# Subtracting the low halves of all split weights on VectorE instead of GpSimd, in a two-layer hybrid decoder kernel

## The chip, the cores and the metric

The kernel runs on one core of a Trainium2 chip. The metric is the device time of one execution in microseconds (us); of several runs the median is given. TensorE is PE in the profile, VectorE is DVE, ScalarE is ACT, GpSimd is POOL, SyncE is SP. PEld is TensorE's weight load.

## The reference

Two layers of a decoder trunk, 512 tokens of width 1024, all in float32. Per layer:

```python
h = rmsnorm(x, norm_g)
proj = h @ w_in                          # 1024 x 11168
a_b, a_c, a_x, a_z, c_q, c_kv, k_pe, b_z, dq, dk, dv, c_z, gate_pre = split(proj)
# A: gated depthwise convolution over 3 tokens
y_a = a_b * (conv_b + sum(up[tap] * conv_w[tap])) * silu(a_z)      # up: shifted a_c * a_x
# B: causal latent attention, 8 heads: q from c_q, k and v from c_kv, rotary key k_pe
y_b = attention(rope(rmsnorm(rmsnorm(c_q) @ w_uq)), rmsnorm(rmsnorm(c_kv) @ w_ukv)) * silu(b_z)
# C: dilated window attention, 3 groups of 8 heads (dilation 1, 4, 16), merged by their log-sums
y_c = dilated(rmsnorm(dq), rmsnorm(dk), dv) * silu(c_z)
merged = sum(sigmoid(gate_i) * (y_i @ w_out_i) for i in (a, b, c))
x = x + merged @ w_o
```

## The kernel before

Every product with a weight matrix is made of three matmuls on split numbers: a float32 value is a high half (a copy rounded to fp32r) and a low half (the value minus its high half). `mm3` (L123 to L128) issues hi·hi, hi·lo and lo·hi. The activations' halves are `hhi` and `hlo` (8 slices of 128x512); the weights come tile by tile.

A weight tile is fetched and split by `split_weights` (L108 to L122). SP issues the DMA into `wraw` (5 buffers, 128x1024), ACT copies it into `whi` (L120, 5 buffers), and another engine subtracts `whi` from `wraw` into `wlo` (L121, 5 buffers). Which engine that is, is chosen by `pool=`. Without the argument it is POOL (`W_POOL = 1`); this holds for all projection tiles through `proj_t` (conv tiles, z tiles, gate tiles), for the `w_out` tiles of the gates and for `w_o`: 136 tiles of 128x1024. The four tiles of 128x768 of each dilated group (24 groups) go to POOL for q in `G_POOL = (0, 2)` and to DVE for the others. The low-rank tiles (128x832) and those of the latent attention are on DVE.

POOL has more work. In layer 0 it adds the squares of x into `acc` (L210), where DVE does it in layer 1. It subtracts the odd slices of `hlo` (L290), the low halves of v (L434), and it scales: k rows (L437), probabilities (L480), the dilated q and k (L596).

The order of PE's instructions is written out by hand. `filler()` yields projection steps (conv tiles, four z tiles, 12 dilated groups, a last conv tile, four z tiles, the gates), and the main line of the layer places a number of them (`F_LORA`, `F_P1` and others) between the small steps of the latent attention, so that PE has matmuls while the other engines normalise and do the softmax. The queues of DVE, ACT, POOL and SP are ordered by the scheduler from priorities, `split_weights` being given 250 steps ahead (`W_AHEAD`), except for the first loads of layer 0, whose DVE, ACT and SP orders are by hand too (from L264). Each engine works through its queue in order.

Steps that come up below, in the order of the program:

- Layer 0's start: `take_chunk` splits x (L211, L212) and sums its squares (L210); `row_scale` sums over partitions on PE (L254), reads that on DVE (L257), and takes the reciprocal root by small DVE steps (`rsqrt`, L98 to L106); PE then spreads the result over rows by L284, and DVE makes h from it (L287).
- The latents: `lat` is normalised (L320, L321) and transposed by PE (L345).
- The latent attention's q and k: `mla_p1` ends with a root and a scaling on DVE (L428), and PE transposes them (L455). Its softmax: DVE L476 and L479, POOL L480, PE L491.
- The convolution's taps on DVE: L823 to L839.
- A dilated group: squares summed on DVE (L590), a root, the scaling on POOL (L596), and PE's transposes (L608).

Of the kernel before, what the change touches and what calls it, by code (L numbers as in the profile page):

```python
# [14 lines left out]
P = 128  # L15
S = 512
# [7 lines left out]
FAR = 1e30  # L24
HIGHEST = 3e38
W_AHEAD = 250
W_POOL = 1
G_POOL = (0, 2)
C8, C2, W_RAW, W_BUF = 2, 38, 5, 5

F_LORA, F_P1, F_P2, F_MLA, F_TAIL, N_TAIL = 24, 6, 10, 1.2, 5.0, 28
# [16 lines left out]
def hybrid_kernel(ctx: ExitStack, tc: tile.TileContext, a: dict):  # L48
    nc = tc.nc
# [7 lines left out]

    ctx.enter_context(tc.manual_schedule(engines={mybir.EngineType.PE}))
    uid = [0]
    wcount = [0]  # L60
    wlast = [None]

    def nm(s):
# [12 lines left out]
    def small(shape, tag, bufs=2):  # L76
        return sp.tile(shape, F32, tag=tag, name=nm(tag), bufs=bufs)
# [15 lines left out]
    hhi = hp.tile([P, KD, S], F32R, name="hhi")  # L93
    hlo = hp.tile([P, KD, S], F32R, name="hlo")
# [10 lines left out]
            nc.vector.tensor_tensor(out=t, in0=t, in1=y, op=ALU.mult)  # L105
            nc.vector.scalar_tensor_tensor(out=y, in0=t, scalar=1.5, in1=y, op0=ALU.add, op1=ALU.mult)  # L106

    def split_weights(n, dmas, pool=None, parts=1):  # L108
        with tc.high_priority(offset=max(0, min(W_AHEAD, tc.cur_priority - base[0]))):
            raw = wp.tile([P, 1024], F32, tag="wraw", name=nm("wraw"), bufs=W_RAW)  # L110
            for lo_, hi_, view, src in dmas:
                wlast[0] = nc.sync.dma_start(view(raw[:, lo_:hi_]), src)
            hi = wp.tile([P, 1024], F32R, tag="whi", name=nm("whi"), bufs=W_BUF)
            lo = wp.tile([P, 1024], F32R, tag="wlo", name=nm("wlo"), bufs=W_BUF)
            wcount[0] += pool is None
            on_pool = wcount[0] % W_POOL == 0 if pool is None else pool
            eng = nc.gpsimd if on_pool else nc.vector
            for i in range(parts):
                c = slice(i * n // parts, (i + 1) * n // parts)
                nc.scalar.copy(hi[:, c], raw[:, c])  # L120
                eng.tensor_sub(lo[:, c], raw[:, c], hi[:, c])  # L121
        return hi, lo  # L122

    def mm3(out, lhs, rhs, start, stop):
# [67 lines left out]
                after_weights(dma)  # L192
        return prm, ropeg

    def new_x(first=False):

        return {"x": [], "hi": [], "lo": [], "acc": small([P, S], "acc", 1), "first": first}

    def take_chunk(X, k, prm):
        src = X["x"][k]  # L200
        hi, lo = t2([P, S], F32R), t2([P, S], F32R)
        X["hi"].append(hi)
        X["lo"].append(lo)
        g = prm[:, O_NORM + k:O_NORM + k + 1]
        if k == 0:
            nc.scalar.activation(X["acc"], src, AF.Square)
        else:
            sq = t2([P, S])
            nc.scalar.activation(sq, src, AF.Square)
            (nc.gpsimd if X["first"] else nc.vector).tensor_add(X["acc"], X["acc"], sq)  # L210
        nc.scalar.activation(hi, src, AF.Copy, scale=g)  # L211
        nc.vector.scalar_tensor_tensor(out=lo, in0=src, scalar=g, in1=hi, op0=ALU.mult, op1=ALU.subtract)  # L212

# [4 lines left out]
    for _ in range(N_WAKE):  # L218
        nc.tensor.matmul(ps[:, :P], wake, wake, start=True, stop=True)

    X = new_x(first=True)
    base = [1 << 40]

    for l in range(DEPTH):
# [6 lines left out]
        wl = {}  # L231

        def lora_w(k):
            n = W_LORA
            dmas = [(0, 2 * n, lambda t: t.rearrange("p (k n) -> p k n", k=2), w_in[:, k:k + 2, C_LORA:C_LORA + n])]
            if l == 0 and k == 0:
                dmas = [(i * n, (i + 1) * n, lambda t: t, w_in[:, i, C_LORA:C_LORA + n]) for i in range(2)]
            wl[k // 2] = split_weights(2 * n, dmas, pool=False, parts=len(dmas))

        def lora(k0, k1):  # L240
            for k in range(k0, k1):
# [43 lines left out]
        for k in range(KD):  # L285
            h32 = t2([P, S])
            nc.vector.scalar_tensor_tensor(out=h32, in0=X["x"][k], scalar=prm[:, O_NORM + k:O_NORM + k + 1],  # L287
                                           in1=psr, op0=ALU.mult, op1=ALU.mult)
            nc.scalar.copy(hhi[:, k], h32)
            (nc.gpsimd if k % 2 else nc.vector).tensor_sub(hlo[:, k], h32, hhi[:, k])  # L290
        lora(n1, n2)
        if l == 0:
            base[0] = tc.cur_priority
# [74 lines left out]
        mla = {}  # L368

        def mla_prep_w(p):  # L370

            o = 0 if p % 2 else 768
            dmas = [(o, o + 256, lambda t: t, w_ukv[:, p * 256:(p + 1) * 256])]
            if p % 2 == 0:
                dmas.insert(0, (0, 768, lambda t: t.rearrange("p (k n) -> p k n", k=2),
                                w_uq[:, :, p * 192:(p + 2) * 192]))
            mla[p] = {"w": split_weights(o + 256, dmas, pool=False)}

        def mla_p1(p):
            m = mla[p]  # L380
# [173 lines left out]
        w_dil = w_in[:, :, C_DIL:C_DIL + 4608].rearrange("p k (s n) -> p k s n", s=3)  # L554
        dil = {}

        def dil_group(p, g):
            if g == 0:
                bias = sp.tile([P, 2, S], F32, tag="bias", name=nm("bias"), bufs=1)
                after_weights(nc.sync.dma_start(bias, a["bias"][2 * p:2 * p + 2].rearrange("h p n -> p h n")))  # L560
                dil[p] = {"bias": bias, "qkt": [], "v": [], "nat": []}
            m = dil[p]
            c0 = g * 512 + p * P
            wq = []
            for q in range(4):
                wq.append(split_weights(768, [
                    (k * 384, k * 384 + 384, lambda t: t.rearrange("p (s n) -> p s n", s=3),
                     w_dil[:, 2 * q + k, :, c0:c0 + P]) for k in range(2)], pool=q in G_POOL))
            both = t8([P, 2, NCH, 256])
            nat, sq = both[:, 0], both[:, 1]  # L570
            vt = t2([P, NCH, P])
            m["nat"].append(nat)
            m["v"].append(vt)

            def evac(c, ps):
                nc.scalar.copy(nat[:, c], ps[:, 0:256])
                nc.scalar.copy(vt[:, c], ps[:, 256:384])

            yield from proj_n(wq, 384, evac)
            if g == 0:  # L580

                vscr = dp.tile([S, P], F32, tag="vscr", name=nm("vscr"))
                nc.sync.dma_start(vscr.rearrange("(r p) d -> p r d", p=P), vt)
                nc.sync.dma_start(vt, vscr.rearrange("(p c) d -> p c d", p=P))
            s2 = small([P, 16], "s16a")
            v2 = small([P, 16], "s16b")
            r2 = small([P, 16], "s16c")
            for c in (0, 2):
                nc.scalar.activation(sq[:, c:c + 2], nat[:, c:c + 2], AF.Square)
                nc.vector.reduce_sum(s2[:, 4 * c:4 * c + 8], sq[:, c:c + 2].rearrange("p c (h d) -> p (c h) d", d=64), axis=AX.X)  # L590
            nc.vector.tensor_scalar(out=v2, in0=s2, scalar1=1.0 / 64, scalar2=EPS, op0=ALU.mult, op1=ALU.add)
            rsqrt(r2, v2, [P, 16])
            nv = nat.rearrange("p c (h d) -> p (c h) d", d=64)
            eng = nc.gpsimd if NV_POOL else nc.vector
            for i in (0, 8):
                eng.tensor_tensor(out=nv[:, i:i + 8], in0=nv[:, i:i + 8],  # L596
                                  in1=r2[:, i:i + 8].unsqueeze(2).to_broadcast([P, 8, 64]), op=ALU.mult)
# [353 lines left out]
        if not last:  # L951
            prm, ropeg = load_params(l + 1, later=True)
            X = new_x()
# [106 lines left out]
```

## Time and profile before

| | before |
|---|---|
| median of 3 runs | 1499.07 us (1498.89 to 1502.35) |
| profiled execution | 1497.07 us, its span 1495.3 us |
| mean granted TensorE clock | 0.988 of full speed |
| PE busy | 1451.1 us (97%) |
| DVE busy | 797.4 us (53%) |
| ACT busy | 699.3 us (47%) |
| POOL busy | 559.5 us (37%) |
| DMA queue q1 | 32.3% of 16 engines' span |

The span is the part of the execution that the profiler's events cover. Busy time is the time in which an engine has an instruction of its own running. That includes time in which the running instruction is held up, so a long duration of a small instruction is itself a sign of waiting. The figure in brackets at the end of a timeline row is the idle time before it and what ended it.

### The profile page before, as it was taken

The numbers are of one execution on the slowest core, as the hardware profiler recorded it, in microseconds if no ns is written. First come the engines' busy times: TensorE is split into PE (matmuls) and PEld (weight loads), VectorE is DVE, ScalarE is ACT, GpSimd is POOL, SyncE is SP. The second block draws the span as 40 slices with busy tenths as digits, with TensorE's granted clock in tenths as the row PEclk, the third lists the DMA queues.
The fourth block names the chain that finished last, engine by engine and source line by source line (L and its number), as shares of the span: only waits on it lengthen the run. The fifth ranks groups of instructions, "written<-read, shape, count | busy, mean of one in ns | idle before, by whom it ended". The sixth has DMA issues, their size and how long they took to land. (4 is left out here: it accounts for less than half of the span.)

```text
span 1495.3 us, 21490 instructions
## 1 busy us (share of the span) xinstructions
PE 1451.1 (97%) x7838; PEld 1272.1 (85%) x7838; DVE 797.4 (53%) x2120; ACT 699.3 (47%) x1600; POOL 559.5 (37%) x348
## 2 busy tenths in 40 slices
PE   8989999999999999999999899999999999999998
PEld 8777899999888878888898778999999878788887
DVE  7757776556464742221665767756474746412221
ACT  4545566647464532232444455657565544322220
POOL 6434243232225434444243433332222434344441
PEclk8999999999999999999999999999999999999999
DMA  8131223234243333333532311234233433233322
GB/s 242 50 95 47 53 68 82 76 85 115 54 124 99 87 85 96 91 104 106 171 101 74 92 36 43 67 85 115 66 92 106 109 91 86 85 99 96 106 81 85
DMA packets 235706, 136.34 MB, mean 91 GB/s; under 512 B 18000, under 2 KB 227280, under 8 KB 235600
## 3 DMA queue, kind: packets, MB, share of 16 engines
q1 hardware_dynamic: 235600, 134.96, 32.3%
q8 instruction: 62, 1.02, 0.3%
q14 instruction: 44, 0.36, 0.1%
HBM read 128.45 MB, written 6.49 MB: 90 GB/s over the span
## 5 line engine op out<-in xcount | busy, mean ns | idle before, releaser
L121 POOL TENSOR_TENSOR wlo<-wraw,whi 128x1024 fp32r<-128x1024 f32 (+1 forms) x184 | 424.7, 2311 | 627.8 <-ACT whi L120 607.2
L120 ACT CAST whi<-wraw 128x1024 fp32r<-128x1024 f32 (+4 forms) x249 | 235.3, 949 | 360.5 <-issue 195.0
L126 PE MATMUL pj<-hhi,whi 128*128 128x512 f32 x760 | 307.8, 405 | 0.2
L127 PE MATMUL pj<-hlo,whi 128*128 128x512 f32 x760 | 298.8, 393 | 0.0
L128 PE MATMUL pj<-hhi,wlo 128*128 128x512 f32 x760 | 298.7, 393 | 0.0
L126 PE MATMUL pj<-whi,hhi 128*128 128x384 f32 x768 | 272.2, 354 | 0.0
L128 PE MATMUL pj<-whi,hlo 128*128 128x384 f32 x768 | 258.4, 336 | 0.0
L127 PE MATMUL pj<-wlo,hhi 128*128 128x384 f32 x768 | 257.6, 335 | 0.0
L128 PEld LDWEIGHTS pj<-hhi,wlo 128*128 128x128 f32 x760 | 143.8, 189 | 31.3
L126 PEld LDWEIGHTS pj<-hhi,whi 128*128 128x128 f32 x760 | 144.3, 190 | 28.1 <-issue 1.4
L127 PEld LDWEIGHTS pj<-hlo,whi 128*128 128x128 f32 x760 | 144.4, 190 | 24.3 <-POOL hlo L290 0.3
L879 DVE SCALAR_TENSOR_TENSOR c<-c,sc 128x512 f32<-128x512 f32 x48 | 32.7, 684 | 239.9 <-PE sc L128 239.9
L126 PEld LDWEIGHTS pj<-whi,hhi 128*128 128x128 f32 x768 | 145.0, 189 | 5.7 <-issue 2.1
L127 PEld LDWEIGHTS pj<-wlo,hhi 128*128 128x128 f32 x768 | 145.2, 189 | 0.6
L128 PEld LDWEIGHTS pj<-whi,hlo 128*128 128x128 f32 x768 | 144.4, 188 | 0.0
L674 ACT ACTIVATE c<-c,e 128x128 f32<-128x128 f32 (+1 forms) x192 | 79.9, 417 | 46.6 <-DVE e L671 46.6
L121 DVE TENSOR_TENSOR wlo<-wraw,whi 128x768 fp32r<-128x768 f32 (+3 forms) x65 | 77.8, 1197 | 42.4 <-ACT whi L120 25.5
L480 POOL TENSOR_SCALAR c<-c,mst 128x128 f32<-128x128 f32 (+1 forms) x64 | 35.5, 555 | 134.9 <-DVE mst L479 100.2
L596 POOL TENSOR_TENSOR c<-c,s16c 128x512 f32<-128x512 f32 x48 | 49.1, 1043 | 91.3 <-DVE s16c L106 91.3
L126 PE MATMUL sc<-c,whi 128*128 128x512 f32 x192 | 75.5, 393 | 0.0
L128 PE MATMUL sc<-c,wlo 128*128 128x512 f32 x192 | 74.9, 390 | 0.0
L127 PE MATMUL sc<-c,whi 128*128 128x512 f32 x192 | 74.8, 390 | 0.0
(201 smaller groups left out, 2367.1 us busy)
## 6 DMA issues: line engine op xcount, KB each, us to landing
wraw<-w_in SPq DMA_DIRECT2D x96, 512.0 KB, 3.7
wraw<-w_in SPq DMA_DIRECT2D x192, 192.0 KB, 2.8
wraw<-w_o SPq DMA_DIRECT2D x16, 512.0 KB, 4.2
bias<-bias SPq DMA_DIRECT2D x8, 512.0 KB, 3.5
wraw<-w_out_a SPq DMA_DIRECT2D x8, 512.0 KB, 3.3
wraw<-w_out_b SPq DMA_DIRECT2D x8, 512.0 KB, 3.3
wraw<-w_out_c SPq DMA_DIRECT2D x8, 512.0 KB, 3.4
wraw<-w_in SPq DMA_DIRECT2D x7, 416.0 KB, 3.7
```

The costliest lines, as they stand in the source:

```text
L120: nc.scalar.copy(hi[:, c], raw[:, c])
L121: eng.tensor_sub(lo[:, c], raw[:, c], hi[:, c])
L126: nc.tensor.matmul(out, lhs[0], rhs[0], start=start, stop=False)
L127: nc.tensor.matmul(out, lhs[0], rhs[1], start=False, stop=False)
L128: nc.tensor.matmul(out, lhs[1], rhs[0], start=False, stop=stop)
L480: nc.gpsimd.tensor_scalar(out=pr[:, :n_], in0=pr[:, :n_], scalar1=st[:, 3:4], scalar2=1.0, op0=ALU.mult, op1=ALU.mult)
L596: eng.tensor_tensor(out=nv[:, i:i + 8], in0=nv[:, i:i + 8], in1=r2[:, i:i + 8].unsqueeze(2).to_broadcast([P, 8, 64]), op=ALU.mult)
L674: nc.scalar.activation(dst, dst, AF.Exp, bias=mc, scale=-1.0, accum_out=sc_)
L879: nc.vector.scalar_tensor_tensor(out=ths[e], in0=ths[e], scalar=1.0, in1=ps, op0=ALU.add, op1=ALU.mult)
```

## The change

The low halves of all split weights are subtracted on DVE: the argument `pool=` and the constants `W_POOL` and `G_POOL` are gone. So are the `first` flag of `new_x`, by which layer 0's sums of squares went to POOL, and the choice of POOL for the odd slices of `hlo`. POOL keeps L434, L437, L480 and L596 (by the numbering of before) and the fills.

```diff
-    def split_weights(n, dmas, pool=None, parts=1):
+    def split_weights(n, dmas, parts=1):
...
-            wcount[0] += pool is None
-            on_pool = wcount[0] % W_POOL == 0 if pool is None else pool
-            eng = nc.gpsimd if on_pool else nc.vector
             for i in range(parts):
                 c = slice(i * n // parts, (i + 1) * n // parts)
                 nc.scalar.copy(hi[:, c], raw[:, c])
-                eng.tensor_sub(lo[:, c], raw[:, c], hi[:, c])
+                nc.vector.tensor_sub(lo[:, c], raw[:, c], hi[:, c])
...
-            (nc.gpsimd if X["first"] else nc.vector).tensor_add(X["acc"], X["acc"], sq)
+            nc.vector.tensor_add(X["acc"], X["acc"], sq)
...
-            (nc.gpsimd if k % 2 else nc.vector).tensor_sub(hlo[:, k], h32, hhi[:, k])
+            nc.vector.tensor_sub(hlo[:, k], h32, hhi[:, k])
...
-                     w_dil[:, 2 * q + k, :, c0:c0 + P]) for k in range(2)], pool=q in G_POOL))
+                     w_dil[:, 2 * q + k, :, c0:c0 + P]) for k in range(2)]))
```

PE's instructions and their order are the same in both. POOL's queue goes from 329 to 130 rows and DVE's from 2000 to 2206; the 199 instructions are 184 of L121, 8 of L290 and 7 of L210. ACT's copies and SP's loads shift by a few places. The lines of the changed kernel are numbered lower: L121 is L115 there, and what stands behind it in the file is lower by 6.

DVE's queue in layer 0's start, before. L121 is the last low-rank tile's subtraction; L257 reads the sum of squares, and L104 to L106 are the root, which ends with the second L106; L287 needs the result through PE's L284.

```order
L121 TENSOR_TENSOR wlo_195<-wraw_192,whi_194 128x832
L305 TENSOR_TENSOR rt_370<-cos_76,ropeg_107 128x128 x2
L212 SCALAR_TENSOR_TENSOR c_52_199<-c_44_183,prm_106,c_51_198 128x512
L257 TENSOR_SCALAR nv_274<-tr_269 128x4
...
L101 TENSOR_SCALAR rs_i_277<-nv_274 128x4
L306 TENSOR_TENSOR rt_370<-sin_77,ropeg_107 128x128
L102 TENSOR_SCALAR nr_275<-rs_i_277 128x4
L104 SCALAR_TENSOR_TENSOR rs_t_278<-nr_275,nv_274 128x4
...
L106 SCALAR_TENSOR_TENSOR nr_275<-rs_t_278,nr_275 128x4
L287 SCALAR_TENSOR_TENSOR c_60_320<-c_9_104,prm_106,tr_315 128x512
```

And now:

```order
L115 TENSOR_TENSOR wlo_195<-wraw_192,whi_194 128x832
L204 TENSOR_TENSOR acc_96<-acc_96,c_53_200 128x512
L206 SCALAR_TENSOR_TENSOR c_52_199<-c_44_183,prm_106,c_51_198 128x512
L251 TENSOR_SCALAR nv_274<-tr_269 128x4
L299 TENSOR_TENSOR rt_370<-cos_76,ropeg_107 128x128
...
L102 TENSOR_TENSOR rs_t_278<-rs_t_278,nr_275 128x4
L103 SCALAR_TENSOR_TENSOR nr_275<-rs_t_278,nr_275 128x4
L115 TENSOR_TENSOR wlo_429<-wraw_426,whi_428 128x1024
L101 SCALAR_TENSOR_TENSOR rs_t_278<-nr_275,nv_274 128x4
...
L103 SCALAR_TENSOR_TENSOR nr_275<-rs_t_278,nr_275 128x4
L115 TENSOR_TENSOR wlo_461<-wraw_458,whi_460 128x1024
L115 TENSOR_TENSOR wlo_502<-wraw_499,whi_501 128x1024
L115 TENSOR_TENSOR wlo_543<-wraw_540,whi_542 128x1024
L281 SCALAR_TENSOR_TENSOR c_60_320<-c_9_104,prm_106,tr_315 128x512
```

The two L305 pairs no longer stand ahead of the last L212, the sum of squares (L204) does; one weight subtraction (`wlo_429`) lies inside the root, and three more (`wlo_461`, `wlo_502`, `wlo_543`) between the root and the first L281 (was L287). On POOL those four were rows of its own queue.

DVE's queue ahead of the first scaling of q in layer 0, before: the end of a conv tile's taps (L837) and the sums from which the root of `mla_p1` is taken (L418 to L101).

```order
L837 SCALAR_TENSOR_TENSOR c_111_601<-c_110_600,prm_106,c_111_601 128x256
L837 SCALAR_TENSOR_TENSOR c_111_601<-c_110_600,prm_106,c_111_601 128x2x96
L837 SCALAR_TENSOR_TENSOR c_111_601<-c_110_600,prm_106,c_111_601 128x2x28
L837 SCALAR_TENSOR_TENSOR c_111_601<-c_110_600,prm_106,c_111_601 128x2x3
L418 TENSOR_REDUCE s24a_623<-c_142_758 128x8
L333 TENSOR_TENSOR c_145_777<-c_116_621,rt_370 128x256
...
L422 TENSOR_SCALAR s24b_624<-s24a_623 128x24
L335 TENSOR_TENSOR c_116_621<-c_145_777 128x4x2x16
```

And now:

```order
L831 SCALAR_TENSOR_TENSOR c_111_601<-c_110_600,prm_106,c_111_601 128x256
L115 TENSOR_TENSOR wlo_951<-wraw_948,whi_950 128x1024
L831 SCALAR_TENSOR_TENSOR c_111_601<-c_110_600,prm_106,c_111_601 128x2x96
...
L831 SCALAR_TENSOR_TENSOR c_111_601<-c_110_600,prm_106,c_111_601 128x2x3
L412 TENSOR_REDUCE s24a_623<-c_142_758 128x8
L327 TENSOR_TENSOR c_145_777<-c_116_621,rt_370 128x256
...
L833 TENSOR_TENSOR c_111_601<-pj_746,c_111_601 128x512
L416 TENSOR_SCALAR s24b_624<-s24a_623 128x24
L115 TENSOR_TENSOR wlo_1078<-wraw_1075,whi_1077 128x1024
L98 TENSOR_SCALAR rs_i_764<-s24b_624 128x24
```

Two weight subtractions, `wlo_951` and `wlo_1078`, which were on POOL, now lie in this chain, the first inside the taps, the second between L416 (was L422) and the root's first step L98 (was L101); the tap's product L833 (was L839) comes ahead of the root.

DVE's queue at the second conv tile's taps, in the softmax stretch of layer 0, before (L479 is a reciprocal of the softmax, L181 a low half of the probabilities, `s24d` the second root of `mla_p1`):

```order
L827 TENSOR_TENSOR c_159_865<-pj_954,c_159_865 128x512
L102 TENSOR_SCALAR s24d_931<-rs_i_990 128x8
L828 TENSOR_SCALAR c_160_866<-c_159_865,prm_106 128x512
L104 SCALAR_TENSOR_TENSOR rs_t_991<-s24d_931,s24b_930 128x8
L837 SCALAR_TENSOR_TENSOR c_160_866<-c_159_865,prm_106,c_160_866 128x384
...
L479 RECIPROCAL mst_1052<-mst_1052 128x1
L181 TENSOR_TENSOR c_203_1039<-tr_1060,c_202_1038 128x2x128
L106 SCALAR_TENSOR_TENSOR s24d_931<-rs_t_991,s24d_931 128x8
```

And now:

```order
L821 TENSOR_TENSOR c_159_865<-pj_954,c_159_865 128x512
L99 TENSOR_SCALAR s24d_931<-rs_i_990 128x8
L115 TENSOR_TENSOR wlo_1380<-wraw_1377,whi_1379 128x1024
L101 SCALAR_TENSOR_TENSOR rs_t_991<-s24d_931,s24b_930 128x8
L473 RECIPROCAL mst_1052<-mst_1052 128x1
...
L102 TENSOR_TENSOR rs_t_991<-rs_t_991,s24d_931 128x8
L822 TENSOR_SCALAR c_160_866<-c_159_865,prm_106 128x512
L103 SCALAR_TENSOR_TENSOR s24d_931<-rs_t_991,s24d_931 128x8
```

`wlo_1380` comes in behind L99 (was L102), and the first tap L822 (was L828) now stands behind the reciprocal L473 (was L479) and behind the next L175 (was L181) and not ahead of them.

## Rows read from the trace of the kernel before

**Rows 1.** Page, part 1: busy time, share of the span, instructions of each engine.

```profile
PE 1451.1 (97%) x7838; PEld 1272.1 (85%) x7838; DVE 797.4 (53%) x2120; ACT 699.3 (47%) x1600; POOL 559.5 (37%) x348
```

**Rows 2.** Waits: who waited for whom, us in total, times, longest.

```profile
PE tr L455 <- DVE c L428: 10.5, 4, 4.1
PE tr L608 <- POOL c L596: 9.7, 11, 1.9
PE tr L284 <- issue: 4.8, 1, 4.8
PE tr L491 <- DVE s24d L106: 3.8, 2, 1.9
PE tr L345 <- DVE c L320: 3.6, 1, 3.6
...
ACT whi L120 <- PE pj L127: 124.8, 44, 5.2
```

**Rows 3.** Stretches: from:to, length, busy (instructions) PE, PEld, DVE, ACT, POOL, clock, DMA.

```profile
100.00:300.00 200.00, 194.44 (x1164) 178.19 (x1164) 134.14 (x399) 124.81 (x326) 70.24 (x71) 0.99 0.25 67
575.00:755.00 180.00, 180.00 (x796) 149.17 (x795) 52.09 (x67) 56.18 (x70) 71.28 (x29) 1.00 0.40 120
```

**Rows 4.** Groups by form: count, busy us, mean ns, idle before and its releasers.

```profile
L121 POOL TENSOR_TENSOR wlo<-wraw,whi 128x1024 fp32r<-128x1024 f32 x136 | 335.5, 2470 | 406.7 <-ACT whi L120 388.8 <-issue 12.6 <-DMA wraw<-w_in 3.4
L121 POOL TENSOR_TENSOR wlo<-wraw,whi 128x768 fp32r<-128x768 f32 x48 | 89.2, 1859 | 221.1 <-ACT whi L120 218.5 <-DMA wraw<-w_in 2.1 <-ACT jw L694 0.5
```

**Rows 5.** DVE's timeline, subtractions with POOL idle: start us, us, what.

```profile
45.57 1.21 DVE L121 TENSOR_TENSOR wlo<-wraw,whi 128x1024 fp32r<-128x1024 f32 x1
46.70 0.28 DVE L332 TENSOR_TENSOR c<-c,rt 128x128 f32<-128x128 f32 x1
...
170.80 0.95 DVE L121 TENSOR_TENSOR wlo<-wraw,whi 128x768 fp32r<-128x768 f32 x1
```

**Rows 6.** POOL's timeline, two places where it subtracts weights.

```profile
20.70 10.70 POOL L121 TENSOR_TENSOR wlo<-wraw,whi 128x1024 fp32r<-128x1024 f32 x4
...
92.72 2.39 POOL L121 TENSOR_TENSOR wlo<-wraw,whi 128x1024 fp32r<-128x1024 f32 x1 [0.82 <-ACT whi L120]
```

**Rows 7.** DVE's timeline, five places that ran beside such a subtraction on POOL.

```profile
57.92 2.50 DVE L320 TENSOR_SCALAR c<-c,lr 128x256 f32<-128x256 f32 x1
...
87.45 5.38 DVE L837 SCALAR_TENSOR_TENSOR c<-c,prm,c 128x384 f32<-128x384 f32 x8
...
93.35 2.04 DVE L333 TENSOR_TENSOR c<-c,rt 128x256 f32<-128x256 f32 x1
...
122.47 2.72 DVE L828 TENSOR_SCALAR c<-c,prm 128x512 f32<-128x512 f32 x1
...
366.66 1.80 DVE L698 TENSOR_TENSOR jz<-jw,e 128x8 f32<-128x8 f32 x1
```

**Rows 8.** DVE's timeline in layer 0's start, ahead of the root.

```profile
21.21 3.18 DVE L121 TENSOR_TENSOR wlo<-wraw,whi 128x832 fp32r<-128x832 f32 x1
24.32 4.87 DVE L305 TENSOR_TENSOR rt<-cos,ropeg 128x128 f32<-128x128 f32 x2
29.12 2.83 DVE L212 SCALAR_TENSOR_TENSOR c<-c,prm,c 128x512 fp32r<-128x512 f32 x1
31.87 0.15 DVE L257 TENSOR_SCALAR nv<-tr 128x4 f32<-128x4 f32 x1
```

**Rows 9.** PE's timeline, around the start's wait.

```profile
20.89 1.93 PE L254 MATMUL tr<-ones,acc 128*128 128x1 f32 x8
...
29.29 0.40 PE L128 MATMUL p<-whi,c 128*128 128x416 f32 x1
34.44 2.05 PE L284 MATMUL tr<-ident,nr 128*128 128x128 f32 x8 [4.75 <-issue]
```

**Rows 10.** Stretches behind two of PE's waits, columns as in rows 3.

```profile
34.00:37.00 3.00, 2.56 (x11) 2.57 (x12) 0.78 (x3) 0.00 (x0) 0.00 (x0) 0.50 0.18 50
37.00:40.00 3.00, 3.00 (x10) 2.88 (x9) 2.87 (x5) 2.43 (x5) 0.72 (x1) 0.50 0.00 0
42.00:46.00 4.00, 4.00 (x20) 3.30 (x19) 3.86 (x6) 2.48 (x5) 1.91 (x2) 1.00 0.01 2
100.00:103.00 3.00, 3.00 (x10) 2.49 (x10) 1.71 (x3) 0.68 (x1) 0.81 (x2) 0.50 0.00 0
```

More of the change, by code (lines that the diff above doesn't have):

```diff
@@ L26 @@
 W_AHEAD = 250
-W_POOL = 1
-G_POOL = (0, 2)
 C8, C2, W_RAW, W_BUF = 2, 38, 5, 5
@@ L59, in hybrid_kernel @@
     uid = [0]
-    wcount = [0]
     wlast = [None]
@@ L193, in load_params, with new_x @@
         return prm, ropeg
-    def new_x(first=False):
-        return {"x": [], "hi": [], "lo": [], "acc": small([P, S], "acc", 1), "first": first}
+    def new_x():
+        return {"x": [], "hi": [], "lo": [], "acc": small([P, S], "acc", 1)}
     def take_chunk(X, k, prm):
@@ L219, in hybrid_kernel @@
         nc.tensor.matmul(ps[:, :P], wake, wake, start=True, stop=True)
-    X = new_x(first=True)
+    X = new_x()
     base = [1 << 40]
@@ L237, in lora_w @@
                 dmas = [(i * n, (i + 1) * n, lambda t: t, w_in[:, i, C_LORA:C_LORA + n]) for i in range(2)]
-            wl[k // 2] = split_weights(2 * n, dmas, pool=False, parts=len(dmas))
+            wl[k // 2] = split_weights(2 * n, dmas, parts=len(dmas))
         def lora(k0, k1):
@@ L376, in mla_prep_w @@
                                 w_uq[:, :, p * 192:(p + 2) * 192]))
-            mla[p] = {"w": split_weights(o + 256, dmas, pool=False)}
+            mla[p] = {"w": split_weights(o + 256, dmas)}
         def mla_p1(p):
```

## The prediction

> **What bounds the kernel now.** The page's busy times come first [rows 1]: PE is busy for 97% of the span, DVE for 53%, POOL for 37%. So only two things can change the time: the 3% in which PE waits, and what the clock does behind such waits. The stretches show where [rows 3]: from 575 to 755 us PE is busy 180.00 of 180, and no faster subtraction can help; from 100 to 300 us it is busy 194.44 of 200 while DVE is busy 134.14. The waits by partner [rows 2] say on whom: PE's five largest are 10.5 + 9.7 + 4.8 + 3.8 + 3.6 = 32.4 us, at L455, L608, L284, L491 and L345. Each is the end of a chain of small DVE steps, or of one POOL step behind such a chain. POOL's own subtractions are on none of these waits.
>
> Why are those chains late? DVE's timeline answers: small instructions take about 2 us when POOL subtracts a weight tile at the same time [rows 7]. From two free rows [rows 5], 1024 columns in 1.21 us and 768 in 0.95, a DVE instruction costs about 0.17 + 0.00102 per column (an estimate; 128 columns would be 0.30, and L332 has 0.28). L333 with 256 columns would then take 0.43 and took 2.04; the POOL row beside it runs from 92.72 to 95.11, and L333 ends at 95.39, when POOL is through [rows 6, 7]. So DVE stands until POOL's instruction ends. L320, L828 and L698 look the same, and of the eight taps L837 (1021 columns together, 2.4 us by the estimate) the row has 5.38 [rows 7]. On POOL a tile costs 2.47 us, on DVE 1.21 [rows 4, 5].
>
> **The change, part by part.** The sum is made against the profiled execution, 1497.07 us, which is 2.0 below the median of 1499.07; I add these 2.0 at the end.
>
> *The work itself.* DVE gets 136 x 1.21 + 48 x 0.95 + 15 x 0.69 (512 columns by the estimate) = 165 + 46 + 10 = 221 us [rows 4, 5]. It goes from 797 to at most 1018 us, 68% of the span, and the stalls it loses come off that: it does not become the bound. In the gates' stretch a weight tile is 24 matmuls, 24 x 180/796 = 5.4 us of PE; DVE has 52.09 us there and gets at most 29 tiles (POOL's whole count) x 1.21 = 35, so 87 of 180 [rows 3]. That costs nothing; the cover is five buffers of 5.4 us. If a subtraction had to wait at the head of DVE's queue, that cover would be used up first.
>
> *Layer 0's start (L284, 4.8).* L257 could not run before L212, which ended at about 31.9; PE's sums were there at 20.89 + 1.93 = 22.82 [rows 8, 9]. L121 (832 columns, 1.02 by the estimate) took 3.18, two L305 took 4.87, L212 took 2.83, all beside POOL's 10.70 us of four subtractions [rows 6, 8]. By the new order one sum (0.69) and L206 (0.69) follow the last low-rank tile: from 21.21, even if nothing earlier is faster, 21.21 + 1.02 + 0.69 + 0.69 = 23.6. From L257 to L284 it took 34.44 - 31.87 = 2.57; now two L299 (0.28 each) and one subtraction (1.13, its distance to L332) lie in it: 23.6 + 2.6 + 0.6 + 1.1 = 27.9. PE's matmuls ahead of L284 end at 29.69. So the whole wait goes: **-4.8**. [...] What is late next is `hlo`, 16 instructions of 0.69 and a subtraction on DVE, about 12 us; PE reaches the first one that needs it after the last low-rank step and a whole tile (24 matmuls), about 10 us, and takes another 5 over the eight slices, so it just holds.
>
> *L455 (10.5; twice about 4.1, twice about 1.2).* The stalls in front of it are 5.38 - 2.4 = 3.0 and 2.04 - 0.43 = 1.6; the new order puts two subtractions of 1.13 in: 4.6 - 2.3 = 2.3 off each long one, and half of each short one: -4.6 - 1.2 = **-5.8**. Behind the long one 10 matmuls started in 3 us at clock 0.50, where 15 would at 1.00 [rows 10]: 1.0 each, **-2.0**, if the rest of the wait is short enough to leave the clock up. Bounds -12.5 (all) and 0 (the subtractions have to wait for their `whi`).
>
> *L491 (3.8).* L828 took 2.72 (0.69 free), with L479 behind it, which releases the scaling on POOL that PE waits for. L828 now stands behind it and one subtraction ahead: 2.72 - 1.13 = 1.6 of 1.9, and taps moved behind L479 give the rest: **-3.8**; the small waits just behind it, which no row here holds, at -1. Bounds -6 and 0.
>
> *L345 (3.6).* L320 gives back 2.50 - 0.43 = 2.1 [rows 7], two subtractions (2.3) come in, of which the first stands ahead of the root's first step and is taken to cost half: **-1.0** here and **-1.0** in layer 1, between -3.6 and +2.
>
> *L608 (9.7 in 11).* The chain loses stalls like L698's (1.80 against 0.18) and gets up to two subtractions of 768 columns (0.87 each, by distance): about even, but the sums of squares also stand earlier in the queue, and the scaling L596 on POOL itself has no subtraction ahead of it in POOL's queue any more. **-3**, between -9.7 and +6.
>
> *New waits.* DVE's queue is in order: a subtraction whose `whi` is not there holds all that follows it. ACT's `whi` waited 44 times for PE to release its buffer, 124.8/44 = 2.8 us each [rows 2]. POOL's remaining steps (L480, L596) will in turn wait for a DVE subtraction, up to 1.2 us. Nothing in the rows says how often; none would be 0, and five times 2.8 is 14. I take a value in the lower half, because those 124.8 us were waits for a PE that was itself busy: **+6**.
>
> Sum: -4.8 - 1.8 - 5.8 - 2.0 - 3.8 - 1.0 - 2.0 - 3 + 6 = -18.2; 1497.07 - 18.2 + 2.0 = 1480.9, rounded to **1480**.
>
> [...] L332 starts at 46.70 and the subtraction before it ends at 45.57 + 1.21 = 46.78 [rows 5]: the next instruction starts 0.08 us before the end, so a subtraction costs the engine 1.13, not more than its row. [...]
>
> **The rivals.**
>
> *Even.* The subtractions in the chains (two ahead of L455, two ahead of L345, one ahead of L491) take what the stalls give back, and only the start's 6.6 remains, with new waits of 4 against it: 1499.07 - 2.6 = 1496.5. For it: the count of subtractions in the chains; against it: each costs 1.13 and a stall costs 1.6 to 2.2. [...]
>
> *Nearly all waits go.* 32.4 + 3.8 (clock) + the small ones, 38 in all: 1499.07 - 38 = 1461. For it: DVE would have half the length of each obstacle; against it: the chains are long without any stall (the root alone is some 2.3 us of the start's 2.57).
>
> *Slower: DVE blocked at the head of its queue.* A subtraction waits for `whi`, `whi` for PE, and a step that PE waits for stands behind it. On POOL such a wait held up little: L480 and L596 alone. Price 2.8 us each time PE has no filler left [rows 2]. The attention stretches, some 250 us of each layer, get at the mean rate of 184 subtractions in 1495 us about 60 of them. It decides from 24/2.8 = 9 of 60 on (24 is the gain without new waits); twelve give 1499.07 - 24 + 34 = 1509. For it: an in-order queue and 44 such waits. Against it: those waits are ACT's, mostly where PE is fully busy.
>
> *The change does not do what it says:* excluded by the order, where POOL has no weight subtraction left.
>
> **How the numbers follow.** Forecast 0.64; nearly all waits 0.12; even 0.12 and its variant 0.02; slower 0.10. A measurement of this kernel can tell about 0.3% from no change, 4.5 us: under 1494.6 is faster, 0.64 + 0.12 = 0.76; the even cases, 0.14, are the same; 0.10 slower. The range leaves out the slower case and the better half of "nearly all": 1460 to 1501; the upper end is the forecast with L455, L491, L345 and L608 all at nothing, and new waits of 14: 1499.07 - 6.6 + 14 is 1506, of which a part lies outside.
>
> **What would show it.** Right: no small DVE step of over 1.5 us is left in the attention stretches; the wait at L284 is gone, and the clock from 30 to 40 us is near 1.00; L455 waits about 2 us where it waited 4.1; DVE is busy less than 1018 us, by what the stalls gave back, and POOL less than 559.5 - 335.5 - 89.2 = 135 [rows 1, 4]. Wrong: waits of PE for `wlo` or of DVE for `whi` of 2 us and more with idle PE behind them; PE waiting within the first AX tile for `hlo`; a new wait in the gates' stretch.

## The result, and the profile after

The changed kernel takes **1459.42 us** (median of 4 runs, 1458.85 to 1460.98) against 1499.72 for the kernel before on the same chip (1498.89 to 1502.35): a ratio of 0.9734, with a 95% interval of 0.972 to 0.9749. It is faster by 40 us. The prediction said 1480, in a range of 1460 to 1501: right in direction, half the size, and the measured time lies just outside the range, where the rival "nearly all waits go" (1461) stood.

The profiled execution took 1459.06 us. Its page, part 1, beside [rows 1]:

```profile
PE 1437.4 (99%) x7838; PEld 1264.9 (87%) x7838; DVE 866.5 (59%) x2319; ACT 699.4 (48%) x1600; POOL 118.4 (8%) x149
```

DVE took on 199 instructions and only 69 us of busy time. Its groups by form show what they cost, beside [rows 4]:

```profile
L115 DVE TENSOR_TENSOR wlo<-wraw,whi 128x1024 fp32r<-128x1024 f32 x140 | 172.6, 1236 | 200.5 <-ACT whi L114 195.3 <-DMA xr<-xT 4.2
L115 DVE TENSOR_TENSOR wlo<-wraw,whi 128x768 fp32r<-128x768 f32 x96 | 90.8, 955 | 31.6 <-ACT whi L114 30.6
L602 PE MATMUL tr<-ident,c 128*128 128x128 f32 x192 | 26.0, 274 | 0.4 <-POOL c L590 0.4
```

The prices of the prediction hold (1.236 and 0.955 us against 1.21 and 0.95). Their sum, 222 us, is more than the moved work adds to DVE's busy time: in the run below without the 184 weight subtractions DVE is busy for 672.3 us, so they add 866.5 - 672.3 = 194 us. Part of the 28 between them is that 1544 of DVE's 2319 instructions start before the end of the one ahead, by a median of 0.08 us (L204 below at 19.06, with L115 running to 19.14): 184 x 0.08 is 15 (an estimate). The other 15 moved instructions (L204 and L284) add about 9 more, at 0.61 us each by distance (an estimate: 0.69 less 0.08). DVE's remaining instructions then take 672.3 - 9 = 663 us; in the kernel before the same instructions took 797.4 [rows 1]. **About 134 us of DVE's busy time before were stalls**, 0.73 us for each of POOL's 184 weight subtractions. They can be seen one by one: 82 instructions of DVE took over 1.5 us in the kernel before; in the changed kernel 4 do, all of them weight subtractions of 1024 columns (1.68 and 1.76). The waits, beside [rows 2]:

```profile
PE tr L449 <- DVE c L422: 4.6, 2, 2.3
PE tr L449 <- DVE c L175: 2.8, 4, 0.8
PE tr L485 <- DVE c L175: 2.2, 4, 0.8
PE tr L339 <- DVE c L314: 1.6, 2, 1.3
PE pj L120 <- DVE c L817: 1.3, 1, 1.3
...
PE tr L602 <- POOL c L590: 0.4, 2, 0.2
```

The line of L284 (now L278) and those of the roots ahead of L491 (now L485) no longer appear, L608 (now L602) fell from 9.7 to 0.4, L455 (now L449) from 10.5 to 4.6 and some small ones. The start on DVE and PE, beside [rows 8, 9]:

```profile
18.12 1.02 DVE L115 TENSOR_TENSOR wlo<-wraw,whi 128x832 fp32r<-128x832 f32 x1
19.06 0.68 DVE L204 TENSOR_TENSOR acc<-acc,c 128x512 f32<-128x512 f32 x1
19.66 0.74 DVE L206 SCALAR_TENSOR_TENSOR c<-c,prm,c 128x512 fp32r<-128x512 f32 x1
22.53 0.16 DVE L251 TENSOR_SCALAR nv<-tr 128x4 f32<-128x4 f32 x1 [2.13 <-PE tr L248]
...
26.03 0.16 DVE L103 SCALAR_TENSOR_TENSOR nr<-rs_t,nr 128x4 f32<-128x4 f32 x1
26.11 3.50 DVE L115 TENSOR_TENSOR wlo<-wraw,whi 128x1024 fp32r<-128x1024 f32 x3
```

```profile
27.91 0.39 PE L122 MATMUL p<-whi,c 128*128 128x416 f32 x1
28.14 1.05 PE L278 MATMUL tr<-ident,nr 128*128 128x128 f32 x8
```

The low-rank tile takes 1.02 and no longer 3.18; the root is done at 26.2, with 1.9 us to spare before PE asks for it at 28.14. And the stretches behind the waits, beside [rows 3, 10] (columns as there):

```profile
28.00:34.00 6.00, 6.00 (x32) 5.64 (x32) 4.87 (x7) 3.81 (x8) 0.00 (x0) 1.00 1.07 296
89.00:92.00 3.00, 3.00 (x18) 2.39 (x17) 1.96 (x3) 2.53 (x4) 0.15 (x1) 1.00 0.01 3
...
575.00:755.00 180.00, 180.00 (x792) 153.15 (x791) 82.17 (x114) 56.89 (x72) 0.00 (x0) 0.99 0.38 115
```

The granted clock stays at 1.00 behind L278, and behind L449 in layer 0, where PE now waits 2.28 and not 4.05 us. The gates' stretch is as full as before. In layer 1 PE waits for L449 just as long, and there the clock falls to 0.50 behind it:

```profile
88.20 0.61 PE L449 MATMUL tr<-ident,c 128*96 128x128 f32 x4 [2.28 <-DVE c L422]
809.03 0.61 PE L449 MATMUL tr<-ident,c 128*96 128x128 f32 x4 [2.28 <-DVE c L422]
...
810.00:813.00 3.00, 3.00 (x11) 2.34 (x10) 1.41 (x3) 1.75 (x3) 0.00 (x0) 0.50 0.04 8
```

In another profiled execution of the same kernel (timed once more, below) it is the other way round: 0.51 behind L449 in layer 0 and 1.00 in layer 1.

```profile
90.00:93.00 3.00, 3.00 (x10) 2.27 (x10) 1.32 (x2) 1.48 (x2) 0.42 (x1) 0.51 0.00 0
812.00:815.00 3.00, 3.00 (x17) 2.46 (x16) 1.96 (x3) 2.42 (x4) 0.40 (x1) 1.00 0.03 8
```

In each of the two executions the clock fell behind one of the two waits; what decides which stays open.

PE's order is the same in both, so the same matmul can be found in both traces, and the difference of its start times says where the gain lies:

| up to the matmul that started before at | starts after at | gained in this stretch | what lies in it |
|---|---|---|---|
| 40.30 | 31.90 | 8.4 | L284, and the clock |
| 56.11 | 49.35 | -1.6 | the new wait on L817 |
| 90.21 | 80.32 | 3.1 | L345 |
| 115.25 | 101.19 | 4.2 | L455, the long wait |
| 150.10 | 133.38 | 2.7 | L491 and just behind it |
| 299.99 | 282.94 | 0.3 | the short waits of L455, and new ones |
| 558.66 | 534.28 | 7.3 | the dilated groups, L608 |
| 800.04 | 775.68 | 0.0 | the gates |
| 828.71 | 802.51 | 1.8 | L345 in layer 1 |
| 850.31 | 821.48 | 2.6 | L455 in layer 1, where the clock falls again |
| 890.20 | 858.67 | 2.7 | L491 in layer 1 |
| 1039.79 | 1008.02 | 0.2 | as in layer 0 |
| 1300.93 | 1262.84 | 6.3 | the dilated groups in layer 1 |
| 1489.97 | 1451.88 | 0.0 | the gates, the output |

The spans of the two profiled executions differ by 38.1 us. By part 1 of their pages PE's idle time makes 24.4 of it (44.2 to 19.8, the span less the busy time) and its busy time 13.7 (1451.1 to 1437.4), while the mean granted clock rose from 0.988 to 0.998.

### The profile page after: what moved, and what is told of

Read it like the earlier page. It is cut to its first block, busy times and chain, and to the rows that moved or that the text cites. A ratio compares the mean times of both kernels' runs of the same rounds, so it can differ in the third digit from the quotient of the medians.

```text
span 1457.2 us, 21491 instructions
## 1 busy us (share of the span) xinstructions
PE 1437.4 (99%) x7838; PEld 1264.9 (87%) x7838; DVE 866.5 (59%) x2319; ACT 699.4 (48%) x1600; POOL 118.4 (8%) x149
## 3 DMA queue, kind: packets, MB, share of 16 engines
q8 instruction: 62, 1.02, 0.3%
## 4 chain that ended last, share of the span: by engine, by line
PE 88%; DVE 8%; ACT 1%; issue 1%; DMA 1%; POOL 0%; SPq 0%; DVEq 0%; ACTq 0%; POOLq 0%
PE pj L120 22%; PE pj L122 21%; PE pj L121 21%; PE sc L120 4%; PE sc L121 4%; PE sc L122 4%; PE pv L766 2%; DVE wlo L115 2%; PE tr L602 1%; PE sc L657 1%; PE pv L502 1%; PE tr L735 1%; PE p L120 1%; PE p L122 1%; PE p L121 1%
## 5 line engine op out<-in xcount | busy, mean ns | idle before, releaser
L115 DVE TENSOR_TENSOR wlo<-wraw,whi 128x1024 fp32r<-128x1024 f32 (+4 forms) x249 | 273.4, 1103 | 232.5 <-ACT whi L114 226.1
L121 PE MATMUL pj<-hlo,whi 128*128 128x512 f32 x760 | 297.2, 391 | 0.0
L121 PE MATMUL pj<-wlo,hhi 128*128 128x384 f32 x768 | 257.2, 335 | 0.0
L121 PEld LDWEIGHTS pj<-hlo,whi 128*128 128x128 f32 x760 | 143.4, 189 | 24.3 <-DVE hlo L284 0.3
L121 PEld LDWEIGHTS pj<-wlo,hhi 128*128 128x128 f32 x768 | 144.8, 189 | 0.4
L590 POOL TENSOR_TENSOR c<-c,s16c 128x512 f32<-128x512 f32 x48 | 51.0, 1084 | 370.9 <-DVE s16c L103 351.7
L121 PE MATMUL sc<-c,whi 128*128 128x512 f32 x192 | 74.7, 389 | 0.0
L665 DVE CUSTOM_DVE_ANT_0 c<-sc,bias 128x128 f32<-128x128 f32 (+1 forms) x192 | 52.9, 319 | 33.0 <-PE sc L651 19.1
L584 DVE TENSOR_REDUCE s16a<-c 128x8 f32<-128x512 f32 x48 | 32.7, 682 | 61.7 <-ACT c L583 61.3
L472 ACT ACTIVATE c<-c,mst 128x128 f32<-128x128 f32 (+1 forms) x64 | 36.0, 563 | 60.9 <-DVE mst L470 60.9
```

Source lines behind the costliest of these rows:

```text
L115: nc.vector.tensor_sub(lo[:, c], raw[:, c], hi[:, c])
L121: nc.tensor.matmul(out, lhs[0], rhs[1], start=False, stop=False)
L472: nc.scalar.activation(pr[:, :n_], pr[:, :n_], AF.Exp, bias=st[:, 0:1], scale=-1.0, accum_out=st[:, 2:3])
L590: eng.tensor_tensor(out=nv[:, i:i + 8], in0=nv[:, i:i + 8], in1=r2[:, i:i + 8].unsqueeze(2).to_broadcast([P, 8, 64]), op=ALU.mult)
L665: nc.vector.tensor_tensor_reduce(dst, src, b, op0=ALU.add, op1=ALU.min, scale=1.0, scalar=HIGHEST, accum_out=mc)
```

## The experiments

Theory A: a DVE instruction stands while POOL's subtraction reads SBUF, and the gain is the end of these stalls. Rival B: the gain comes from the shorter subtraction (low halves and buffers earlier) and from DVE's other order. Lines of the runs' kernels are a few higher than in the changed kernel where code was put in.

**POOL's reading brought back, DVE's work left.** Edits of the changed kernel: in the first run on the 184 tiles, in the second on all 236 tiles of these widths, and in the third with fills in place of subtractions.

```diff
+    def split_weights(n, dmas, parts=1, again=False):
...
+            if again or n == 1024 and len(dmas) == 1:
+                nc.gpsimd.tensor_sub(raw[:, :n], raw[:, :n], hi[:, :n])
...
+                     w_dil[:, 2 * q + k, :, c0:c0 + P]) for k in range(2)], again=q in (0, 2)))
```

```diff
+            if n in (768, 1024):
+                nc.gpsimd.tensor_sub(raw[:, :n], raw[:, :n], hi[:, :n])
```

```diff
+            if n in (768, 1024):
+                for _ in range(2):
+                    nc.gpsimd.memset(raw[:, :n], 0.0)
```

> The changed kernel, and POOL subtracts once more, in place and for nobody, on just the 184 tiles that the change took from it. So POOL does the work of before, and DVE that of the changed kernel. Theory A: DVE's busy time goes from 866 us to that plus the stalls of before; those were 797 - (866 - 222) = 153 us (222: the moved instructions at their free prices), so about 1019; the time is the 57 us that all stalls are worth (before against the kernel without any moved subtraction, 1499.7 - 1442.6) above 1459: 1516, and more than that if stalls and added work pile up on DVE, up to 1560. Rival B (low halves and buffers come earlier, another order): 1459 to 1470.

> The changed kernel, and beside every 128x768 and 128x1024 weight tile POOL subtracts once more, in place, a result that nobody uses, after DVE is done with the tile. Theory A (the gain is the end of stalls: a DVE instruction with two inputs in SBUF stands while POOL's subtraction runs): DVE's busy time climbs from 866 us by some 100 to 150, small DVE steps of about 2 us are back in the attention stretches, and the time returns to 1490 to 1515, no better than the kernel before, though every weight's low half is still made by DVE. Rival B (the gain is that the subtraction is shorter on DVE, so that low halves and buffers come earlier, and that DVE's queue has another order): 1459 to 1465, since neither has changed.

> As the run in which POOL subtracts once more, but POOL only fills the tile twice with zeros at the same place: it is busy at the same moments and holds the buffer of the raw weights as long or about so, and reads nothing. Theory A, if it is POOL's reading that stops DVE: DVE's busy time stays near 866 us and the time at 1457 to 1465. If any work of POOL stops DVE, or if it is the later release of the raw buffer that costs: as in the other run, 1480 or more, and then with or without the stalls of 2 us on DVE, which tells these two apart.

Measured: 1548.3 us (ratio to before 1.0323, 1.0307 to 1.0338), 1598.1 (1.0663, 1.0647 to 1.0679) and 1475.15 (0.9838, 0.9824 to 0.9853). The first is within its range. The second is far beyond 1490 to 1515: with 52 more tiles on POOL, DVE was busy for 1083.9 us, 217 more than in the changed kernel. The third lies between its two ranges. The pages' busy times, of 184 subtractions and of the fills:

```profile
PE 1468.7 (95%) x7838; PEld 1280.8 (83%) x7838; DVE 1020.0 (66%) x2319; ACT 699.4 (45%) x1600; POOL 557.3 (36%) x333
```

```profile
PE 1445.3 (98%) x7838; PEld 1268.9 (86%) x7838; DVE 882.3 (60%) x2319; ACT 699.0 (47%) x1600; POOL 523.4 (35%) x621
```

POOL is about equally busy in both, the raw buffers are held for its work in both, and DVE has the same instructions; with reading it is busy for 1020.0 us, 153.5 more than in the changed kernel, and without it for 882.3. That 1019 was expected is in part luck: the 153 of the expectation count each moved subtraction at its whole length, and the stalls of before were about 134. The run loses 89 us against the changed kernel, 57 of them in PE's idle time (77.3 against 19.8) and 31 in its busy time. One place shows the stall. DVE's and POOL's timeline ahead of the root of `mla_p1`, of the run with 184 subtractions:

```profile
93.13 1.22 DVE L115 TENSOR_TENSOR wlo<-wraw,whi 128x1024 fp32r<-128x1024 f32 x1
94.27 3.36 DVE L833 SCALAR_TENSOR_TENSOR c<-c,prm,c 128x192 f32<-128x192 f32 x3
97.55 0.67 DVE L414 TENSOR_REDUCE s24a<-c 128x8 f32<-128x512 f32 x1
...
100.66 2.33 DVE L99 TENSOR_SCALAR s24c<-rs_i 128x24 int32<-128x24 int32 x1
...
94.90 2.52 POOL L117 TENSOR_TENSOR wraw<-wraw,whi 128x1024 f32<-128x1024 f32 x1
100.53 2.42 POOL L117 TENSOR_TENSOR wraw<-wraw,whi 128x1024 f32<-128x1024 f32 x1 [3.11 <-DVE rs_i L98]
```

And of the run with fills:

```profile
86.80 1.21 DVE L115 TENSOR_TENSOR wlo<-wraw,whi 128x1024 fp32r<-128x1024 f32 x1
87.93 1.22 DVE L834 SCALAR_TENSOR_TENSOR c<-c,prm,c 128x192 f32<-128x192 f32 x3
...
88.55 1.97 POOL L118 MEMSET wraw<- 128x1024 f32 x2
```

The same three taps, each with two inputs in SBUF, take 3.36 us beside a subtraction and 1.22 beside the fills. Theory A is shown for such instructions, and rival B falls: low halves were made as in the changed kernel, and DVE's order was its own but for 5 of 2319 places in the first run and 35 in the third. The fills still cost 15.7 us above the changed kernel; PE's waits there at L605 (3.3 us, POOL's scaling) and L452 (7.7) have grown (0.4 and 4.6 in the changed kernel), and the raw buffers are released later, after two fills of 0.955 us (1024 columns) or 0.741 us (768). DVE's busy time rose too, by 15.8 us: in the run with fills the small instructions with one SBUF input at L98, L585 and L99 of the dilated groups took 7.0, 4.7 and 2.6 us longer (24 instructions each). The root's first step in the dilated groups, in the changed kernel and in the run with fills:

```profile
L98 DVE TENSOR_SCALAR rs_i<-s16b 128x16 int32<-128x16 int32 x24 | 3.8, 160 | 0.2
L98 DVE TENSOR_SCALAR rs_i<-s16b 128x16 int32<-128x16 int32 x24 | 10.8, 448 | 0.4
```

Which of these makes up the 15.7 was not tried.

**The three parts of the change alone,** each an edit of the kernel before: `G_POOL = ()`; the wide tiles (`on_pool = False` where no `pool=` is given); and the sums of squares and `hlo` on DVE.

> The kernel before with one part of the change: all four weight tiles of each dilated group are subtracted on DVE, everything else stays on POOL. If the parts add, place by place: PE's waits at L608 go (9.7 us, and some 4 us beside them in the dilated stretches), the other waits stay: 1485, between 1482 and 1490. My prediction's reason (the added subtractions eat what the stalls give back): 1494 to 1500.

> The kernel before with another part of the change: the 136 tiles of 128x1024 are subtracted on DVE; half of the dilated groups' tiles, the sums of squares at the start and the odd slices of hlo stay on POOL. If the parts add: the waits at L284, L345, L455 and L491 shrink as in the changed kernel (-24 in all), those at L608 stay: 1474 to 1480; DVE's stalls of 2 us are gone up to 200 us and are still there between 300 and 450 us. If the three parts only work together (one POOL subtraction anywhere makes DVE late for long): 1485 or more.

> The kernel before with the third part of the change alone: the sums of squares and all slices of hlo on DVE, the weights as before. If the parts add, what is left of the changed kernel's 40 us beside the two other parts (12.4 and 26.1) is about 1 to 2 us: 1496 to 1500. The wait at L284 stays then, since POOL's four weight subtractions still run beside the root. If it was the sums on POOL that made the start late: L284's wait goes and the time is 1491 to 1493.

Measured: 1486.77 (-12.4 to 1499.13 on that chip; 0.9918, 0.9903 to 0.9933), 1473.01 (-26.1; 0.9828, 0.9812 to 0.9845), and 1500.49 (-0.2 to 1500.66; 0.9998, 0.9984 to 1.0013). The parts add: 12.4 + 26.1 + 0.2 = 38.7 of 40.3. PE's waits of the run with the dilated groups alone:

```profile
PE tr L455 <- DVE c L428: 8.1, 2, 4.1
PE tr L284 <- issue: 5.8, 1, 5.8
PE tr L491 <- DVE s24d L106: 3.8, 2, 1.9
PE tr L345 <- DVE c L320: 3.6, 1, 3.6
PE tr L608 <- POOL c L596: 2.8, 4, 0.8
```

L608 went from 9.7 to 2.8 and the long waits stayed, but for L284 (4.8 before, 5.8 here, with the clock at 1.00 ahead of it). Between the two profiled executions (1497.07 and 1488.37) that is 6.9 of 8.7 us. My reason in the prediction, that added subtractions eat there what the stalls give back, is refuted. In the third run L284 still waits (3.6 us): it was mainly the four subtractions on POOL that made the start late, not the sums.

**The gates back on POOL** (70 tiles), an edit of the changed kernel:

```diff
+                gp[0] = d2 > 0
...
+                (nc.gpsimd if gp[0] else nc.vector).tensor_sub(lo[:, c], raw[:, c], hi[:, c])
```

> The changed kernel with one part undone: from the gates' second step on, and in the output projection, the weight tiles (70 of the 184) are subtracted on POOL again. If a stall costs only where PE waits on DVE (theory A with the cover of five buffers): DVE's steps there are stalled again, PE stays busy there, 1457 to 1462. If a subtraction on POOL costs wherever it runs, by its later low half: 70/184 of the gain, some 15 us, is lost: 1474.

Measured 1461.25 (0.9734, 0.9715 to 0.9754), the changed kernel's own ratio. DVE is busy there for 804.5 us, 23.2 more than in the run below that leaves these 70 subtractions out (781.3), so the stalls are back. In this run PE was busy for 180.00 us of the 180 from 575 on and for 150.00 of the 150 from 1290 on; there it made no difference which engine subtracts, and the stalls cost nothing.

**Without moved subtractions,** edits of the changed kernel by `lo = hi` for all 184, for the 48 of the dilated groups, and for the 70 of the gates and the output projection.

> The changed kernel without the 184 subtractions that the change moved: PE takes the high half of those weights in place of the low half, so that part of the computation is left out (its matmuls all stay). It gives what the added work on DVE still costs. By PE's waits that are left in the changed kernel (15.5 us in all) the time can't fall under about 1444. If the moved subtractions cost about what I put down (two ahead of L455, L345, one ahead of L491, 0.9 to 1.1 each): 1447 to 1451. If they hide in DVE's idle time: 1454 to 1459.

> The changed kernel without the 48 moved subtractions of the dilated groups (PE takes the high half in place of the low half there, so that part of the computation is left out). In the changed kernel PE waits 0.4 us at L602, so if the cost lies where PE still waits: 1457 to 1460, no gain. If the 48 load DVE beyond their own stretch: 1452 to 1455.

> The changed kernel without 70 moved subtractions, those of the gates from the second step on and of the output projection (high half in place of the low half there). By the prediction's cover they cost nothing: 1458 to 1461. With the dilated groups' at nothing too, the other 66, in the attention stretches, take all the 17 us.

Measured: 1442.58 (0.9612, 0.9592 to 0.9632), 1453.08 (0.9682, 0.9664 to 0.9701) and 1460.79 (0.9731, 0.9717 to 0.9745). The first is under the 1444 that I had put as the least: I had counted PE's waits alone, and its busy time fell too, from 1437.4 to 1432.5 us. So all stalls (with late low halves, as far as PE met any) were worth 1499.7 - 1442.6 = 57 us, and the moved work takes 17 of them back: none of it in the gates, some 6 in the dilated groups (against 1459.45 for the changed kernel on that chip), the other 10 to 11, as the rest, in the wide tiles of the attention stretches. The 6 is rough: the four runs came as two at a granted clock of 0.995 (1455.3, 1455.8) and two at 1.000 (1450.2, 1450.9). In the run without any of the 184, PE hardly waits:

```profile
PE 1432.5 (99%) x7838; PEld 1263.2 (88%) x7838; DVE 672.3 (47%) x2135; ACT 698.7 (49%) x1600; POOL 113.8 (8%) x149
...
PE tr L488 <- DVE c L178: 1.3, 2, 0.7
PE tr L216 <- POOL c L213: 1.0, 1, 1.0
PE tr L452 <- DVE c L457: 0.5, 2, 0.3
```

**Each subtraction twice on DVE,** an edit of the changed kernel.

> The changed kernel with every subtraction of a 128x768 or 128x1024 tile done twice on DVE (236 more, about 250 us; DVE at some 1115 us, three quarters of the span). As my prediction counted, each subtraction in a chain that PE waits for adds its whole 0.9 to 1.1 us: ten of 1024 columns and some 24 of 768 give 11 + 21 = 32 more, 1491. If most of them run while DVE would wait for ACT or PE anyway: 1465 to 1475. The stalls' theory says nothing against either, but beyond 1500 it would be DVE's load and not the stalls that made the kernel before slow.

Measured 1578.58 (1.0523, 1.0493 to 1.0553): worse than either expectation.

```profile
PE 1477.3 (94%) x7838; PEld 1289.3 (82%) x7838; DVE 1106.6 (70%) x2555; ACT 700.5 (45%) x1600; POOL 125.1 (8%) x149
```

DVE is busy 1106.6 us, 240 more, and the kernel takes 119 us longer: PE's idle time grew by some 75 us (95.3 against 19.8), and its busy time by 40, at a mean granted clock of 0.974 against 0.998. New waits are spread over the attention stretches (L451 13.6 us, the dilated scores' L659 13.5, L604 11.8, and PE for low halves 10.1). The first 194 us of moved work cost 17, the next 240 cost 119: the slack on DVE is nearly used up. By the wording of the expectation this would make load the cause of the slow kernel before; but that one had less load than the changed kernel (797 against 866 us) and took 40 us longer, so load alone does not order the kernels.

**Two tries to go further,** edits of the changed kernel: `F_LORA, F_P2 = 26, 14`, and `W_AHEAD = 120` (twice, the second beside the changed kernel itself).

> The changed kernel with more of PE's filler ahead of two places where it still waits on DVE: F_P2 from 10 to 14 steps (ahead of L449, which waits 2.3 us in each layer) and F_LORA from 24 to 26 (ahead of L339, 1.3 and 0.3). A step is three matmuls, some 0.7 us. If the waits left are chains on DVE that run a little too long, the filler covers them: -4.6 - 1.6 and 1 to 2 of clock, 1452 to 1455. If DVE is short of time as a whole in these stretches, the waits move to the next step of the chain: 1457 to 1460.

> The changed kernel with the weights' splits given 120 steps of priority instead of 250, so that on DVE fewer of them stand ahead of the attention's chains. If it is their place in the queue that costs the 17 us which the moved subtractions still take: 1450 to 1456. If they only move to other places of the same chains: 1457 to 1462. If weights then come late: 1465 and more, with PE waiting for low halves.

> The changed kernel as it is, once more, to stand beside the run with 120 steps of priority on the same chip: 1459 (1457 to 1461).

> The changed kernel with 120 steps of priority for the weights' splits instead of 250, timed against the changed kernel on the same chip. The first run gave 1457.1 beside 1459.4 of another chip's look. If the place in the queue matters: 2 to 3 us under the changed kernel with intervals apart. If not: within 1 us of it.

More filler: 1473.9 (0.9829, 0.9812 to 0.9845), 14 us worse than the changed kernel and outside both expectations. The wait at L449 is down to 2.0, but L485 waits 6.5, the dilated L602 3.8, and a projection 5.3 on ACT's L571: the later steps of the chain met PE's next need later. The order by hand seems to fit the chains as a whole.

Less priority: 1457.08 (0.9712, 0.9698 to 0.9727), then 1456.14 (0.9705, 0.9692 to 0.9718) beside 1459.45 for the changed kernel (0.9721, 0.9708 to 0.9735). It was 2.3 and 3.3 us better by the medians, but the intervals overlap; likely a small gain, not a shown one. It is the fastest full kernel measured here.

## Why the prediction was right in direction and wrong in size

- **The mechanism held.** Stalls of DVE beside POOL's subtractions set the chains PE waits for; prices on DVE, the order, the gates at nothing and POOL's 118 us (under 135) came as said, and DVE stayed far under 1018. Of the signs named for being right, the small steps over 1.5 us and the wait at L284 are gone, and L449 waits about 2 us.
- **L284:** -6.6 forecast (4.8 for the wait, 1.8 for the clock behind it), 8.4 measured. The wait went as worked out; PE reached L278 at 28.14 and not at 29.69, 1.55, which goes with the clock behind L254 (below). No run shows the 1.8 by itself; the two traces show 2.1 in its place, 5.86 us from the start of L284 (34.44 to 40.30) at a clock of 0.52 and 3.76 for the same matmuls in the changed kernel (28.14 to 31.90) at 1.00.
- **L455 and L491:** -7.8 and -4.8 forecast. Measured 4.2 + 2.6 = 6.8 for the long waits, 2.7 + 2.7 = 5.4. The long wait fell by 1.8 in each layer, where 2.3 was forecast; the clock stayed up behind it in layer 0 and fell in layer 1, so "if the rest of the wait is short enough to leave the clock up" came true once in two. The short waits gained about 1 each and lost it to new ones.
- **L345:** -2.0 forecast, 3.1 + 1.8 = 4.9 measured. "Of which the first is taken to cost half" was too dear: it ran (44.27 to 45.49) before the root's inputs were all there, the last of them being read at 45.59.
- **L608: the step that failed.** "About even, ... -3" stood against 7.3 + 6.3 = 13.6, half of what was missing. I set two added subtractions against one stall. DVE's own half of these tiles had been stalled too: a row that I did not use had them at 1.221 us on DVE where 0.955 is the free price. And I took each added subtraction at its whole length, though 48 of them cost some 6 us over 24 groups, a quarter us for a group and an eighth for a tile. The term also had no clock in it: PE's idle time in these stretches fell by 9.6 us, and the other 4.0 are PE's busy time. Part of that is the clock, which stood at the lower level behind L608's wait of 1.86 us in layer 0 of the kernel before:

```profile
L121 DVE TENSOR_TENSOR wlo<-wraw,whi 128x768 fp32r<-128x768 f32 x48 | 58.6, 1221 | 40.3 <-ACT whi L120 23.5 <-issue 16.3
...
443.00:446.00 3.00, 2.66 (x11) 2.26 (x11) 3.00 (x13) 1.28 (x2) 0.77 (x1) 0.50 0.00 0
```

- **New waits:** +6 forecast, the second largest miss: the stretches that hold them gained or lost little (-1.6, 0.3 and 0.2, about 1 lost in all). One of 1.3 us (L817) and some of 0.6 to 0.8 came; the stretch up to 56.11 lost 1.6, the others are mostly in the two stretches that gained 0.3 and 0.2. My rival "DVE blocked at the head of its queue" did not occur: DVE waited 226 us for `whi`, but within 4 us ahead of any wait of PE on DVE by no more than 0.31 us at a time, and PE itself waited 0.4 for `whi`.

Together: 18.2 forecast, 38.0 in the table. Of the 19.8 between them L608 is 10.6, the new waits 4.9, L345 2.9 and the start 1.8 (L491 gave 0.6 more, L455 1.0 less). By kind, PE's waits fell by 24.4 where the sum had 14.4, and its busy time by 13.7 where the sum had 3.8 for the clock; I priced the clock behind L284 and L455 alone. The stalls were worth 57 and the moved work gave back 17; my terms had set the two against each other chain by chain and left 24 before new waits. I had priced five rows of stalls; a sum over all of DVE's instructions could have been had from the trace before: the excess over the median, or over the fastest tenth, of instructions of the same line and shape is 118 or 164 us (an estimate from that trace, by the choice of the free price).

## What to carry to other kernels

When POOL and DVE both read SBUF, sum the excess of every DVE instruction over its free price before costing single chains; the total (here about 134 us, 0.73 per POOL subtraction) shows how much stands in the way, and the waits of PE show where it counts. Work that a scheduler places on DVE cost far less per us than stalls that fall on whatever instruction is next: 194 us of the one took 17, about 134 us of the other 57 (with late low halves). That holds only while DVE has slack: the next 240 us cost 119.

## What was not expected of the hardware

- DVE instructions with one SBUF input were stalled too: L99 (128x24) took 2.33 us in the run with 184 subtractions, 0.17 on average in the changed kernel. Sums over the free axis were not: of the 56 of 512 columns in the kernel before (L418, L590), 14 ran beside a weight subtraction on POOL, at 0.685 us on average against 0.678 for the others.
- The clock behind L254 (eight matmuls of one column) was lower in the kernel before, 0.63 from 22 to 26 us, and 1.00 in the changed kernel from 20 to 26, though PE was never idle around it in either. In other runs with the changed start it was 0.91 (fills) and 0.85 (gates on POOL), and in the run with the dilated groups alone, whose start is that of before, 1.00; so part of the start's extra gain may come and go, and what decides it stays open.

```profile
22.00:26.00 4.00, 4.00 (x14) 3.92 (x15) 4.00 (x2) 1.05 (x1) 4.00 (x2) 0.63 0.29 61
```

```profile
20.00:26.00 6.00, 6.00 (x27) 6.00 (x27) 3.69 (x17) 2.70 (x4) 0.00 (x0) 1.00 0.76 202
```
